# A hybrid attention and convolution block: conv taps as ScalarE products with wide adds, weight sums in place, values two blocks at a time, and seven-product blocks for 6 of 16 pairs

## The chip, the cores and the metric

The kernel runs on one core of one Trainium2 chip. The metric is device time in microseconds (us) of one execution. It is measured as the median of several runs. One more execution is profiled, and all rows of the profile come from that one.

Engine names as in the profile: PE is TensorE (matmul), PEld its weight load, DVE is VectorE, ACT is ScalarE, POOL is GpSimd, SP is SyncE, which issues almost all DMAs.

## The reference

All tensors are float32; the sequence has 256 positions and the model width is 4096.

```
xn = rms_norm(x) * g                                  # (256, 4096)
proj = xn @ w_in                                      # (4096 x 14336)
q, k, v, z_a, a_c, g_c, z_c = split(proj)             # seven parts of 2048
y_a = chunked_attention(q, k, v, rel_table)           # 16 heads of 128, relative bias
y_a = rms_norm(y_a) * silu(z_a)
u   = a_c * sigmoid(g_c)
u   = causal depthwise conv(u, w_dw: 31 taps x 2048 channels) + b_dw
y_c = silu(layer_norm(u)) @ w_pw + b_pw
y_c = rms_norm(y_c) * silu(z_c)
h   = x + concat(y_a, y_c) @ w_out
h   = h + sigmoid(rms_norm(h) @ w_ple_gate + b) * (p @ w_ple)
out = rms_norm(h)
```

## The kernel before

**Products.** Almost all of the time goes into matrix products of a 256-row operand with weights that stream from HBM. A float32 value is split into a high part (rounded to the fp32r type) and a low part (the rest). A product is then three matmuls: high times high, low times high, high times low. For every weight tile of 128 x 1024 values (two column blocks of 512), ACT makes the high part by a cast (`wh`, L197) and DVE makes the low part by a subtraction (`wl`, L198); both are in `parts_of`. PE then reads both.

**`mixed_product`** multiplies the operand by two column blocks at once (2 x 2 outputs of 128 x 512: the 4096 rows of the weight are 16 pairs of 128-row blocks). For a plain pair it issues 2 x 2 x 2 products, that is 24 matmuls. For a pair marked with a star in the order lists (`steady`, `dense`, `early` and so on) it uses a seven-product scheme: 21 matmuls, for which DVE has to form four sums of weight blocks (`ua`, `ub`, L398 to L403) and ACT and DVE have to split these sums too (`uh`, `ul`, through `pair_parts`). The order list `early` marks 4 of 16 pairs.

**Stages.** In order of time: the normalisation and transposition of x together with the first two plain products (block 0 of g and a); then a loop over four blocks g of 512 columns, in which `glu_conv(g + 1)` makes a and g of the next block by one `mixed_product` (in `scaled_pair`) and `heads(g)` makes q and k by another, the values v by a plain `product`, and then runs the attention of four heads; then the layer norm of the convolution (`layer_norm_swish`), the pointwise product, the gates z, the output product, and the gated embedding. The loop over blocks takes about the stretch from 100 to 950 us.

**The convolution** runs on DVE beside these products: `conv_tap` multiplies a 128 x 256 block by one tap's weight and adds it to the accumulator in one instruction (L574; the first tap, with the bias, is L570). There are 4 blocks of 4 x 31 such instructions. They are not issued in one go: they lie in a queue `later`, and `fill(n)` takes n of them after each pair of a product; the input products take 4 per pair, the value product 2.

**Order.** The kernel is recorded by a layer that has its own planner: it may move independent instructions of one engine ahead of others, so the order on an engine is that of the built program and not that of the source. Each engine works strictly through its own order; waits between engines are semaphores.

**Buffers.** Raw weight tiles `wt` have 5 buffers, `wh` and `wl` 3 each, `uh` and `ul` 2 each, the raw sums `ua`/`ub` 2. A DMA for a raw tile is issued (SP) when the tile's last reader is done.

**The layer norm** of the convolution goes over several engines in turn: POOL adds the four blocks and folds them, PE multiplies by a matrix of 1/2048 (the mean, L636), DVE subtracts the mean (`center`, L648), ACT squares (L652), POOL adds and folds the squares (L656, L625, L626), PE makes the variance (L663), and so on. These steps lie in `later` too.

## Time and profile before

| what | value |
|---|---|
| median of 3 runs | 2062.86 us (2062.17 to 2063.23) |
| profiled execution, its own time | 2063.82 us |
| profiled execution, its span | 2061.7 us |
| PE busy | 2034.6 us, 9140 matmuls |
| PEld busy | 1675.2 us |
| DVE busy | 1822.1 us |
| ACT busy | 1152.9 us |
| read from HBM | 406.39 MB |

A row of the groups gives the line, the engine, the operation, the tiles (out<-in), the shapes, the count, then the busy time of the group, the mean duration of one in ns, and the idle time of the engine in front of the group with what ended it. A row of the windows view gives, for one stretch, the busy time (and count) of each engine, the granted TensorE clock, and the share and rate of the DMA engines. A row of the timeline gives start, duration, engine, line, operation and count. Since instructions of one engine overlap a little, the distance between two starts is less than a duration; the distance is what an engine's work adds up from.

### The profile page before, as it was taken

How to read it: one execution, taken by the hardware profiler on the slowest of the kernel's cores; microseconds unless marked ns; L12 is line 12 of the kernel's file. 1: busy time of each engine (PE TensorE's matmuls, PEld its weight loads, DVE VectorE, ACT ScalarE, POOL GpSimd, SP SyncE). 2: the span in 40 equal slices, each digit the busy share in tenths (PEclk: the TensorE clock that was granted, in tenths of full speed). 3: DMA queues.
4: the chain of work that ended last, by engine and by line, in shares of the span. 5: the costliest groups of instructions: out<-in, count | busy, mean ns of one | idle time of the engine just before them, and what ended most of it. 6: DMA issues, size and time to landing. Idle time of an engine off the chain costs nothing.

```text
span 2061.7 us, 25882 instructions
## 1 busy us (share of the span) xinstructions
PE 2034.6 (99%) x9140; PEld 1675.2 (81%) x9140; DVE 1822.1 (88%) x2541; ACT 1152.9 (56%) x1479; POOL 42.9 (2%) x37
## 2 busy tenths in 40 slices
PE   9999999999999999999999999999999999999997
PEld 7888888887888787788888888878888888888886
DVE  7599999899977998875889999899999999999954
ACT  7445535554564535575556656576565666656543
POOL 0000000000000002300000000000000000000000
PEclk9999999999999999999999999999999999999998
DMA  8656665656566665555666666666666656666664
GB/s 291 186 186 201 191 197 184 195 188 188 175 204 185 194 190 164 186 184 195 194 210 202 200 215 197 212 229 206 212 202 206 211 185 192 210 229 210 220 208 166
DMA packets 170331, 412.27 MB, mean 200 GB/s; under 512 B 13006, under 2 KB 16222, under 8 KB 170202
## 3 DMA queue, kind: packets, MB, share of 16 engines
q1 hardware_dynamic: 169914, 410.11, 62.5%
q8 instruction: 71, 1.16, 0.2%
q10 hardware_dynamic: 288, 0.52, 0.1%
q14 instruction: 58, 0.48, 0.1%
HBM read 406.39 MB, written 4.19 MB: 199 GB/s over the span
## 4 chain that ended last, share of the span: by engine, by line
PE 90%; DVE 6%; issue 2%; DMA 1%; ACT 1%; POOL 0%; SPq 0%; ACTq 0%; POOLq 0%; DVEq 0%
PE acc L351 53%; PE acc L210 22%; PE acc_P L351 13%; DVE wl L198 2%; DVE cv L574 1%; PE tmp_ps L156 1%; DVE ul L198 1%; DMA wt<-in_w_in_dram 1%; DMA wt<-in_w_ple_gate_dram 0%; PE tmp_ps L724 0%; PE tmp_ps L739 0%; PE tmp_ps L757 0%; ACT wh L197 0%; DMA xin<-in_x_dram 0%; PE tmp_ps L762 0%
## 5 line engine op out<-in xcount | busy, mean ns | idle before, releaser
L197 ACT CAST wh<-wt 128x1024 fp32r<-128x1024 f32 (+1 forms) x741 | 727.0, 991 | 628.8 <-PE acc L351 319.6
L351 PE MATMUL acc<-wh,big_t 128*128 128x512 f32 x3344 | 1038.8, 391 | 3.4 <-ACT big_t L142 2.9
L198 DVE TENSOR_TENSOR wl<-wt,wh 128x1024 fp32r<-128x1024 f32 (+1 forms) x741 | 850.7, 1159 | 130.2 <-ACT wh L197 127.6
L351 PEld LDWEIGHTS acc<-wh,big_t 128*128 128x128 f32 x3344 | 626.7, 188 | 133.3 <-ACT big_t L142 3.4
L351 PE MATMUL acc<-wl,big_t 128*128 128x512 f32 x1672 | 652.1, 391 | 3.3 <-DVE wl L198 3.2
L210 PE MATMUL acc<-wh,big_t 128*128 128x512 f32 x1248 | 390.2, 393 | 0.0
L351 PEld LDWEIGHTS acc<-wl,big_t 128*128 128x128 f32 x1672 | 314.4, 188 | 71.9 <-DVE wl L198 7.2
L210 PEld LDWEIGHTS acc<-wh,big_t 128*128 128x128 f32 x1248 | 234.9, 189 | 48.2 <-DVE big_t L143 0.2
L210 PE MATMUL acc<-wl,big_t 128*128 128x512 f32 x624 | 243.4, 391 | 0.0
L574 DVE SCALAR_TENSOR_TENSOR cv<-uT,dw,cv 128x256 f32<-128x256 f32 x480 | 214.3, 487 | 1.0
L197 ACT CAST uh<-ub 128x1024 fp32r<-128x1024 f32 x103 | 108.3, 1051 | 113.1 <-DVE ub L403 92.4
L351 PE MATMUL acc_P<-uh,big_t 128*128 128x512 f32 x534 | 163.7, 390 | 0.0
L197 ACT CAST uh<-ua 128x1024 fp32r<-128x1024 f32 x103 | 108.6, 1054 | 63.9 <-DVE ua L399 59.0
L210 PEld LDWEIGHTS acc<-wl,big_t 128*128 128x128 f32 x624 | 117.9, 189 | 24.1
L198 DVE TENSOR_TENSOR ul<-ub,uh 128x1024 fp32r<-128x1024 f32 x103 | 128.2, 1245 | 7.9 <-ACT uh L197 7.1
L198 DVE TENSOR_TENSOR ul<-ua,uh 128x1024 fp32r<-128x1024 f32 x103 | 125.8, 1222 | 0.4
L351 PEld LDWEIGHTS acc_P<-uh,big_t 128*128 128x128 f32 x534 | 99.9, 188 | 21.4 <-ACT uh L197 0.8
L351 PE MATMUL acc_P<-ul,big_t 128*128 128x512 f32 x267 | 103.8, 393 | 0.9 <-DVE ul L198 0.9
L398 DVE TENSOR_TENSOR ua<-wt 128x512 f32<-128x512 f32 x103 | 71.6, 695 | 30.7 <-DMA wt<-in_w_in_dram 17.4
L399 DVE TENSOR_TENSOR ua<-wt 128x512 f32<-128x512 f32 x103 | 70.8, 688 | 4.6 <-DMA wt<-in_w_in_dram 4.3
L403 DVE TENSOR_TENSOR ub<-ub,wt 128x512 f32<-128x512 f32 x103 | 72.2, 701 | 1.2
L402 DVE TENSOR_TENSOR ub<-ua,wt 128x512 f32<-128x512 f32 x103 | 70.9, 688 | 0.2
(199 smaller groups left out, 1349.3 us busy)
## 6 DMA issues: line engine op xcount, KB each, us to landing
wt<-in_w_in_dram SPq DMA_DIRECT2D x447, 512.0 KB, 3.9
wt<-in_w_out_dram SPq DMA_DIRECT2D x128, 512.0 KB, 4.2
wt<-in_w_ple_gate_dram SPq DMA_DIRECT2D x128, 512.0 KB, 4.0
wt<-in_w_pw_dram SPq DMA_DIRECT2D x32, 512.0 KB, 4.3
hc<-in_x_dram SPq DMA_DIRECT2D x8, 512.0 KB, 5.3
wt<-in_w_ple_dram SPq DMA_DIRECT2D x8, 512.0 KB, 4.7
out_dram<-hc SPq DMA_DIRECT2D x16, 256.0 KB, 2.9
xin<-in_x_dram SPq DMA_DIRECT2D x7, 512.0 KB, 8.3
```

Source lines behind the costliest of these rows:

```text
L156: nc.tensor.transpose(pt[:, i * T + h * P : i * T + (h + 1) * P], src[:, h, b * P : (b + 1) * P], ident,)
L197: nc.scalar.copy(wh[:, :kc, :], wt[:, :kc, :]),
L198: nc.vector.tensor_tensor(wl[:, :kc, :], wt[:, :kc, :], wh[:, :kc, :].bitcast(F32), ALU.subtract),
L210: nc.tensor.matmul(acc, a, b[:, k, :], start=kb == 0 and kind == 0, stop=kb == kblocks - 1 and kind == 2,)
L351: nc.tensor.matmul(banks[name], a, b, start=name not in begun, stop=final and ends[name] == n and kind == 2,)
L398: plus(ua[:, 0], w0[:, 0], w0[:, 1])
L399: plus(ua[:, 1], w0[:, 1], w1[:, 1])
L402: plus(ub[:, 0], ua[:, 0], w1[:, 1])
L403: plus(ub[:, 1], ub[:, 0], w1[:, 0])
L574: nc.vector.scalar_tensor_tensor(cv[:, i, :], uT[:, i, k : k + T], dw[:, b, k : k + 1], cv[:, i, :], ALU.mult, ALU.add,)
```

## The change

Five things change.

1. **Convolution.** A tap is no longer one DVE instruction per 128 x 256 block. ACT multiplies each of the four blocks by its tap's weight into a tile `prod` (128 x 4 x n, two buffers), and DVE adds all four at once to the accumulator (`tt`, 128 x 4 x n, n from 255 down to 226). The newest tap, with the bias, is written to the accumulator by ACT directly. The 31 taps of a block are now 32 steps of the queue. In the input products `fill` takes two steps after a plain pair and none after a starred one.
2. **Weight sums in place.** The four sums are written over the raw weight tiles, and the parts of the sums take their buffers from the common `wh`/`wl`, which now have 5 each. The order of the seven products follows.
3. **Values.** v is made for two column blocks at once by `mixed_product` (for g = 0 and g = 2), instead of four plain products, and attention writes its result over v.
4. **Seven products** for 6 of 16 pairs (`early`, and `after_heads` where a product follows an attention) instead of 4 of 16, in all products of the loop over blocks. The sums of x for this cover 6 column blocks instead of 4.
5. **Copies and the layer norm's place.** The PSUM copies of q, k and of the transposed probabilities move from DVE to ACT. The layer norm starts in front of the last q and k product, which takes 8 steps after each plain pair.

In the built program the change has these counts: matmuls of 128 x 512 go from 8619 to 8541; the 496 tap instructions on DVE go away; 496 products of 128 x 256 and less appear on ACT and 120 wide adds on DVE; the starred pairs go from 103 to 129.

```diff
-        return [wpool.tile([P, KC, NB], F32R, tag=tag, name=tag, bufs=3) for tag in ("wh", "wl")]
+        return [wpool.tile([P, KC, NB], F32R, tag=tag, name=tag, bufs=5) for tag in ("wh", "wl")]
...
-    early = units("1 3 5 7 0* 9 2* 11 4* 13 6* 15 8 10 12 14")
+    early = units("1 3 5 0* 7 2* 9 4* 11 6* 13 8* 15 10* 12 14")
+    after_heads = units("1 3 5 7 0* 9 2* 11 4* 13 6* 8* 15 10* 12 14")
...
             w0, w1 = wts
-            ua = upool.tile([P, 2, NB], F32, tag="u", name="ua")
-            ub = upool.tile([P, 2, NB], F32, tag="u", name="ub")
             plus = partial(nc.vector.tensor_tensor, op=ALU.add)
             w0h, w0l = parts_of(w0, 1)[0]
-            plus(ua[:, 0], w0[:, 0], w0[:, 1])
-            plus(ua[:, 1], w0[:, 1], w1[:, 1])
-            uah, ual = pair_parts(ua)
+            plus(w0[:, 0], w0[:, 0], w0[:, 1])
+            plus(w0[:, 1], w0[:, 1], w1[:, 1])
             w1h, w1l = parts_of(w1, 2)[0]
-            plus(ub[:, 0], ua[:, 0], w1[:, 1])
-            plus(ub[:, 1], ub[:, 0], w1[:, 0])
-            ubh, ubl = pair_parts(ub)
+            plus(w1[:, 1], w0[:, 0], w1[:, 1])
+            plus(w1[:, 0], w1[:, 1], w1[:, 0])
+            uah, ual = parts_of(w0, 2)[0]
+            ubh, ubl = parts_of(w1, 2)[0]
...
-    def conv_tap(cv, uT, i, b, k):
-        if k == 0:
-            nc.vector.tensor_scalar(
-                cv[:, i, :], uT[:, i, :T], dw[:, b, 0:1], bdw[:, b : b + 1], ALU.mult, ALU.add
+    def conv_steps(cv, uT, c):
+
+        def scaled(dst, i, n, k, **kw):
+            nc.scalar.activation(
+                dst[:, i, :n], uT[:, i, :n], AF.Identity,
+                scale=dw[:, 4 * c + i, k : k + 1], **kw,
             )
-        else:
-            nc.vector.scalar_tensor_tensor(
-                cv[:, i, :], uT[:, i, k : k + T], dw[:, b, k : k + 1], cv[:, i, :],
-                ALU.mult, ALU.add,
-            )
+
+        def step(k):
+            if waiting:
+                at, n, prod = waiting.pop()
+                tt(cv[:, :, at:], cv[:, :, at:], prod[:, :, :n], ALU.add)
+            if k == PAD:
+                for i in range(4):
+                    scaled(cv, i, T, k, bias=bdw[:, 4 * c + i : 4 * c + i + 1])
+            elif k >= 0:
+                n = T - (PAD - k)
+                prod = taps_pool.tile([P, 4, T], F32, tag="prod", name="prod")
+                for i in range(4):
+                    scaled(prod, i, n, k)
+                waiting.append((PAD - k, n, prod))
+
+        waiting = []
+        return [partial(step, k) for k in range(PAD, -2, -1)]
...
-            sg, gate = scaled_pair(w_in0, o_a + c * NB, o_g - o_a, early, r_x, 4)
+            sg, gate = scaled_pair(
+                w_in0, o_a + c * NB, o_g - o_a, early if c == 1 else after_heads, r_x, (2, 0)
+            )
...
+    def heads(g, splits):
+        last = g == n_g - 1
+        q, k = scaled_pair(
+            w_in0, o_q + g * NB, o_k - o_q, after_heads if last else early, r_x,
+            (8, 0) if last else (2, 0), then=partial(later_memory, splits) if last else None,
+        )
+        qT, kT = to_heads(q, "qT"), to_heads(k, "kT")
+        if g % 2 == 0:
+            v = [act.tile([P, NH, NB], F32, tag="act", name="v") for _ in range(2)]
+            values.extend(scaled_pair(w_in0, o_v + g * NB, NB, early, r_x, (2, 0), dst=v))
...
-        accv = product(w_in0, o_v + g * NB, xT, KD)
-        v = spool.tile([P, NH, NB], F32, tag="hd", name="v", bufs=5)
...
-    xS = [big_tile(upool) for _ in range(2)]
-    for c in range(4):
+    xS = [big_tile(upool) for _ in range(3)]
+    for c in range(6):
```

More of the change, by code (lines that the diff above doesn't have):

```diff
@@ L314, in operand @@
         tiles.append(t)
-    def pair_parts(src):
-        tiles = [upool.tile([P, 2, NB], F32R, tag=tag, name=tag) for tag in ("uh", "ul")]
-        return parts_of(src, 2, tiles)[0]
     def units(text):
@@ L447, in sum_tiles, with scaled_pair @@
         return t, [[t[j][:, h] for j in range(2)] for h in range(NH)]
-    def scaled_pair(w, col, apart, order, r, fills):
-        t, z = sum_tiles()
+    def scaled_pair(w, col, apart, order, r, fills, dst=None, then=None):
+        if dst is None:
+            t, z = sum_tiles()
+        else:
+            t, z = dst, [[dst[j][:, h] for j in range(2)] for h in range(NH)]
         def on_helpers(helper):
@@ L604, in glu_conv @@
             nc.scalar.copy(
[L605 removed]
+                uT[:, 2 * pair : 2 * pair + 2, :], pt.rearrange("q (i t) -> q i t", t=T)
             )
         cv = act.tile([P, 4, T], F32, tag="act", name="cv")
[L608 to L610 removed]
+        later.extend(conv_steps(cv, uT, c))
         conv.append(cv)
@@ L675, in spread @@
                 nc.vector.tensor_scalar(d, ident, st["r"][:, h : h + 1], None, ALU.mult)
-                nc.tensor.matmul(m[:, h * P : (h + 1) * P], mean_w, d, start=True, stop=True)
+                nc.tensor.matmul(m[:, h * P : (h + 1) * P], st["w"], d, start=True, stop=True)
             stat("rs", m[:, :T], float(CW))
@@ L708, in layer_norm_swish @@
             later.extend(partial(swish, c, i) for i in range(4))
-        for c in range(n):
-            later.extend(partial(split, c, i) for i in range(4))
+        return [partial(split, c, i) for c in range(n) for i in range(4)]
     y_a = []
```

80 lines of the change are left out of this document (39 added, 41 removed).

## The prediction

> **What bounds the kernel now.** I read the page first, then the windows of 50 us, the waits of PE, the chain, and the timelines of DVE and ACT.
>
> ```profile
> PE 2034.6 (99%) x9140; PEld 1675.2 (81%) x9140; DVE 1822.1 (88%) x2541; ACT 1152.9 (56%) x1479; POOL 42.9 (2%) x37
> ```
>
> ```profile
> 200.00:250.00 50.00, 49.96 (x221) 41.03 (x220) 50.00 (x74) 27.80 (x30) 0.00 (x0) 1.00 0.64 193
> 250.00:300.00 50.00, 50.00 (x230) 41.46 (x229) 49.63 (x86) 20.01 (x20) 0.00 (x0) 1.00 0.63 196
> ...
> 600.00:650.00 50.00, 50.00 (x226) 41.44 (x225) 34.68 (x40) 26.74 (x30) 0.00 (x0) 1.00 0.66 200
> ```
>
> ```profile
> PEld acc L351 <- DVE wl L198: 7.2, 11, 1.9
> ...
> PEld acc_P L351 <- DVE ul L198: 4.0, 11, 0.9
> ```
>
> ```profile
> 938.64 72.34 PE acc L210 x319
> ```
>
> PE sets the time: 319 matmuls in 72.34 us are 0.2268 us each, and in the loop over blocks it keeps nearly that rate. But DVE is full there too (50.00 and 49.63 of 50 us; in a stretch with few taps left 34.68). PE hardly notices: in the whole run it waits 7.2 + 4.0 us for low parts. Both run side by side at the limit, with some weight tiles made ahead. So whoever gives DVE more work in a stretch than PE has there, and more than the tiles ahead cover, pays on PE.
>
> **Prices.** What an engine's work adds up from is the distance between starts.
>
> ```profile
> 1207.10 1.22 DVE L198 TENSOR_TENSOR wl<-wt,wh 128x1024 fp32r<-128x1024 f32 x1
> 1208.24 0.69 DVE L398 TENSOR_TENSOR ua<-wt 128x512 f32<-128x512 f32 x1
> 1208.84 1.22 DVE L198 TENSOR_TENSOR ul<-ub,uh 128x1024 fp32r<-128x1024 f32 x1
> ```
>
> ```profile
> 177.09 2.06 DVE L574 SCALAR_TENSOR_TENSOR cv<-uT,dw,cv 128x256 f32<-128x256 f32 x5
> ```
>
> ```profile
> 162.14 2.00 ACT L197 CAST wh<-wt 128x1024 fp32r<-128x1024 f32 x2
> ```
>
> ```profile
> L574 DVE SCALAR_TENSOR_TENSOR cv<-uT,dw,cv 128x256 f32<-128x256 f32 x480 | 214.3, 487 | 1.0
> ...
> L461 DVE SCALAR_TENSOR_TENSOR z<-acc,r_x,z 128x512 f32<-128x512 f32 x28 | 19.3, 755 | 3.3 <-PE acc L351 3.3
> ...
> L682 ACT ACTIVATE cv<-cv,prm 128x256 f32<-128x256 f32 x16 | 8.5, 591 | 0.0
> ...
> L570 DVE TENSOR_SCALAR cv<-uT,dw,prm 128x256 f32<-128x256 f32 x16 | 6.4, 417 | 0.2
> ...
> L692 ACT CAST big_t<-cv 128x256 fp32r<-128x256 f32 x16 | 5.2, 405 | 0.0
> ```
>
> A DVE operation on 1024 values takes 1.14 us from start to start, one on 512 takes 0.60; a straight line through both gives 0.07 + n/960. A tap takes 0.40 ((2.06 - 0.49) / 4). Two casts of 1024 take 2.00, so one takes just under 1.0. A wide add isn't in the trace. Its two inputs and shape are those of the 1024 subtraction; with 4 x 241 values on average the line gives 1.07 us. The bounds are 0.60 (the 512 row) and 1.60 (four taps). A product of 256 on ACT lies between the cast of L692 (405 ns) and the swish of L682 (591), that is 0.31 to 0.49 from start to start when the 0.1 us of overlap is taken off; with one per-partition factor where L692 has none and L682 two, I take 0.40.
>
> **The change part by part.**
>
> *Matmuls.* Each starred pair saves three. Nine products with 6 stars replace seven with 4 and four plain ones with none: 54 against 28, 26 x 3 = 78 fewer. PE's path shortens by 78 x 0.2268 = 17.7 us.
>
> *DVE over the loop.* Gone: the taps, 214.3 + 6.4 = 221 us. Added: 120 wide adds, 128; 26 more starred pairs at 4.15 more than a plain one (0.60 for the half tile, 4 x 0.60 for the sums, 3 x 1.14 for the parts make 6.42; a plain pair is 2 x 1.14 = 2.28), 108; final sums and scaling for two more products, about 11; two more column blocks of sums of x, 5; less 19 for the copies that go to ACT. The total grows by about 12 us, while PE loses 17.7. The wide adds pay for the starred pairs and no more.
>
> *Where it lies.* This decides. The source takes 20 steps per product, but in the built program the planner has moved more: 28 adds stand in the first gate product (block 1), 23 in the first q/k product, 9 in the first value product, then 28, 2, 28, 2. In such a product of 28 the middle repeats six times: one plain pair, one starred pair, four adds. On DVE: 2.28 + 6.42 + 4 x 1.07 = 12.98 us. On PE: 45 matmuls, 10.2 us. DVE falls behind by 2.8 each time, 16.6 in six. Before, four repeats with eight taps of 0.40 cost 11.9 against 10.2, 6.8 in four, and that stayed covered.
>
> The cover is the tiles ahead. With five buffers DVE can be four tiles ahead of the one that PE is on: in plain pairs 4 x 12 x 0.2268 = 10.9 us, less one cast and one subtraction (2.1), so 8.8 us. For the starts of the products I added up the built order tile by tile: DVE's work up to each low part, less PE's work up to its first matmul. In the order of before this sum never climbs by more than 7 us in the stretch from 100 to 350 us, which fits a DVE that is full and a PE that doesn't wait. In the changed order it climbs by 20 us in the first gate product and, without a recovery, by 8 more in the first q/k product; then, after a full recovery in the value and gate products, by 22 in the second and by 22 in the third q/k product. Less 8.8 once per climb: 11 + 8 + 13 + 13 = 45 us of waiting on PE. With a cover of 12 it is 35, with 7 it is 55.
>
> *ACT.* In the same products ACT has 6 x 3.4 + 10 x 1.9 for casts, 116 x 0.40 for products and 3 for scaling: 89 us, below DVE's 96. The two buffers of `prod` tie it to DVE's adds, but following one repeat through both orders I find each cast ready as DVE comes to it. Cost nothing; with products at 0.49 ACT would have 99 and would be the bound, 3 to 4 us more in each of the four stretches.
>
> *Weight sums in place.* Same instructions, other order: both sums are formed in front of both casts, so DVE has the other two sums to do while ACT casts. Nothing, while raw tiles arrive in time.
>
> ```profile
> wt<-in_w_in_dram SPq DMA_DIRECT2D x447, 512.0 KB, 3.9
> ```
>
> A raw tile of a starred pair is now held until its sum's low part is made, some 4 us longer (0.60 x 2 + 1.14 x 2 more in front of it), and SP's next load waits for that. The load takes 3.9 us, and a repeat on PE is 10.2; DVE's 8.7 of work in the later stages (no adds) leaves this load about 1 us to spare. I take zero; the rival below prices it.
>
> *Values, copies.* Values are counted above. The copies add 13 us to ACT in places where it has room; attention now needs ACT for one more step, with PE's other matmuls between. Zero.
>
> *Layer norm.* Its place changes. In the last q/k product 8 steps follow a plain pair. In the built order the mean's matmul (L636 before) and the variance's (L663 before) stand 42 full matmuls apart, 9.5 us of PE.
>
> ```profile
> L636 PE MATMUL tmp_ps<-lnsum,mean_w x2: 379/416/454, 838.4 to 838.7; 128*128 128x256 f32 x2
> ```
>
> ```profile
> L648 DVE TENSOR_TENSOR cv<-cv,mu x16: 415/418/2615, 840.4 to 854.5; 128x256 f32<-128x256 f32 x16
> ```
>
> ```profile
> L663 PE MATMUL tmp_ps<-mean_w,sq x4: 250/250/271, 864.8 to 865.2; 128*128 128x1 f32 x4
> ```
>
> ```profile
> 847.71 9.15 POOL L656 TENSOR_TENSOR sq<-sq 128x1024 f32<-128x1024 f32 x2 [44.16 <-ACT sq L652]
> 858.44 2.41 POOL L656 TENSOR_TENSOR sq<-sq 128x1024 f32<-128x1024 f32 x1 [1.58 <-ACT sq L652]
> 860.93 2.15 POOL L625 TENSOR_TENSOR sq<-sq 128x512 f32<-128x512 f32 x1
> 863.16 1.60 POOL L626 TENSOR_TENSOR sq<-sq 128x256 f32<-128x256 f32 x1
> ```
>
> Before, the way from the one to the other took 26.4 us (838.4 to 864.8), with enough matmuls between. In the changed order DVE does its 16 subtractions in one go, so the way shortens: 0.7 for the mean, 2.7 for the first two blocks, 1.1 to square, then POOL's 9.15 + 2.41 + 2.15 + 1.60, together 19.8. PE waits 19.8 - 9.5 = 10 us, in order, and so do the casts that stand behind the squares on ACT. Bounds: 5 (POOL's two long adds at 2.41 each) and 15 (a way as slow as before).
>
> Beside DVE's subtractions POOL needs 9.15 us for two of its adds, and 2.41 for the third. [...]
>
> *Clock.* PE's waits can cost twice.
>
> ```profile
> 500.67 0.33 PE L724 MATMUL tmp_ps<-ident,z 128*128 128x128 f32 x1 [1.35 <-DVE z L461]
> ```
>
> ```profile
> 500.00:505.00 5.00, 4.00 (x18) 3.63 (x19) 4.35 (x7) 0.17 (x1) 0.00 (x0) 0.66 0.27 97
> ```
>
> After a gap of 1.35 us and thin work the granted clock of these 5 us was 0.66: if it was halved, for 3.4 us, which is 1.7 us of PE time. I add one such loss after the layer norm's wait, 1.7; in the stretches where DVE is the bound a slow PE is hidden. [...]
>
> *Waits that go.* Of the 11.2 us that PE waits for low parts before, those outside the four stretches may go: I take 5 off.
>
> *Sum,* against the profiled execution's 2063.8 us: - 17.7 + 45 + 10 + 1.7 - 5 = 2097.8. The median of the runs is 1.0 lower (2062.86), so 2097 us.
>
> **The rivals.**
>
> *Faster: DVE's shortfall stays under the cover.* If a wide add costs 0.65 or less, the repeat costs 11.3, six fall short by 6.6, and that is covered as before. Against it: between the 512 and the 1024 row DVE needs (1.14 - 0.60) / 512 = 1.05 ns a value, whatever the operation's length. For it: the bound 0.60, and a PE that tolerates a full DVE for 250 us now. Then 17.7 and most of 11.2 are gained and the layer norm costs 7: 2063.8 - 17.7 - 11 + 7 - 1 = 2041 us.
>
> *No change:* a cover of 13 (all five tiles) and a layer norm that costs 5 or less, with all old waits gone, bring the shortfall to some 20 to 25 and the time to 2059 to 2067.
>
> *Slower by ACT:* products at 0.49, plus 16: 2113 us.
>
> *Slower by the raw tiles:* if each of the 75 starred pairs behind the loop waits 0.5 us for its load, plus 37: 2134 us. Against it: DVE would have to use up its spare time and its tiles ahead first.
>
> **How the numbers follow.** The forecast has 0.66, its own range 2066 to 2122; ACT 0.05 and the raw tiles 0.04; the faster rival 0.18, spread over 2033 to 2055; no change 0.07. Two in a thousand, 4 us, is about what a measurement of this kernel can tell. Faster 0.18, same 0.07, slower 0.75. The range from 2044 to 2122 leaves out half of the faster rival and the top.
>
> **What would show it.** In the profile after: the wide adds at about 1.1 us; DVE at 50 of 50 in the windows of the first gate and the first three q/k products, with PEld under 40 there and waits of PE and PEld for `wl` of 40 us or more in total; the variance's matmul with a wait of about 10 us for POOL; no loss from about 950 us on, so that the end of the loop moves by as much as the total. Wrong it is if PE's waits for `wl` stay near 11 us, or if the time comes or goes behind the loop.

## The result: slower by 3.1%, and the profile after

| what | before | after |
|---|---|---|
| median of the runs | 2062.52 us (2061.94 to 2063.23, 4 runs) | 2125.84 us (2125.51 to 2126.86, 4 runs) |
| profiled execution, its span | 2061.7 us | 2123.6 us |

The ratio is 1.0308 (95% interval 1.0290 to 1.0326). The forecast of 2097 us had the direction and most of the mechanism, but the change costs 63 us where it said 34; the time lies 4 us above the range.

The page's first part, the windows of 50 us in the same stretches as before, and the waits of TensorE and of its weight loads:

```profile
PE 2043.5 (96%) x9062; PEld 1656.8 (78%) x9062; DVE 1875.3 (88%) x2317; ACT 1392.4 (66%) x2063; POOL 41.6 (2%) x33
```

```profile
150.00:200.00 50.00, 42.30 (x171) 30.85 (x172) 49.34 (x55) 44.88 (x83) 0.00 (x0) 1.00 0.52 165
200.00:250.00 50.00, 49.40 (x221) 39.94 (x219) 49.37 (x55) 44.27 (x77) 0.00 (x0) 1.00 0.58 182
250.00:300.00 50.00, 43.79 (x183) 32.61 (x182) 49.35 (x55) 44.66 (x82) 0.00 (x0) 1.00 0.59 190
500.00:550.00 50.00, 44.81 (x176) 33.08 (x174) 49.58 (x53) 43.64 (x83) 0.00 (x0) 0.94 0.53 168
600.00:650.00 50.00, 50.00 (x229) 41.29 (x230) 41.22 (x50) 30.05 (x41) 0.00 (x0) 1.00 0.49 151
```

```profile
PEld acc_P L347 <- ACT wh L196: 57.6, 43, 3.3
PE acc_P L347 <- ACT wh L196: 38.8, 42, 2.8
PEld acc_P L347 <- DVE wl L197: 20.8, 40, 1.1
```

In the windows of the first gate product and the first two q/k products DVE is at 49.3 to 49.6 of 50, and PE falls to 42 to 45 of 50 in three of the four; in the light product from 600 us on PE is full again. TensorE waits for weight parts of starred pairs (`acc_P`), by name more often for the high part than for the low one. That doesn't make ACT the bound: the high part of a sum can be cast only when DVE has formed the sum. The repeat of a plain pair, a starred pair and four adds shows it, in TensorE's and the page's rows:

```profile
127.21 0.73 PE L347 MATMUL acc_P<-wh,big_t 128*128 128x512 f32 x2 [1.00 <-ACT wh L196]
140.47 0.73 PE L347 MATMUL acc_P<-wh,big_t 128*128 128x512 f32 x2 [1.00 <-ACT wh L196]
153.67 0.73 PE L347 MATMUL acc_P<-wh,big_t 128*128 128x512 f32 x2 [1.00 <-ACT wh L196]
166.79 0.74 PE L347 MATMUL acc_P<-wh,big_t 128*128 128x512 f32 x2 [1.00 <-ACT wh L196]
179.86 0.73 PE L347 MATMUL acc_P<-wh,big_t 128*128 128x512 f32 x2 [1.00 <-ACT wh L196]
```

```profile
L572 ACT ACTIVATE prod<-uT,dw 128x255 f32<-128x255 f32 (+14 forms) x480 | 195.7, 486 | 25.7 <-DVE cv L580 25.0
L580 DVE TENSOR_TENSOR cv<-cv,prod 128x1020 f32<-128x1020 f32 (+14 forms) x120 | 138.4, 1154 | 18.5 <-ACT prod L572 16.5
```

The distance from start to start is 13.1 to 13.3 us where 12.98 was forecast, against 10.2 us of matmuls. Each repeat loses 2.9. A wide add has a mean duration of 1154 ns and a product on ACT one of 486; from start to start both are a little shorter (1.10 to 1.11 us from the adds at 494.65 and 496.37 us to the next operation, 0.40 us for each of 20 products that take 8.05).

To see where TensorE's time goes I added up, from the trace, how far each matmul starts later than 0.227 us after the one ahead of it. Before, this is 33.7 us in all; after, 109.0:

| stretch, us | before | after | forecast, waits that come or go |
|---|---|---|---|
| 100 to 200 (first gate product) | 1.3 | 17.4 | 11 |
| 225 to 300 (first q/k) | 0.5 | 9.9 | 8 |
| 475 to 600 (second q/k and what precedes it) | 4.3 | 21.6 | 13 |
| 675 to 800 (third q/k and what precedes it) | 4.2 | 20.6 | 13 |
| layer norm to last scaling (800 to 950 before, 850 to 1000 after) | 6.2 | 21.5 | 10 |
| from 1000 us on | 7.6 | 10.2 | 0 |

75.3 us more of waiting less 17.7 us of matmuls is 57.6; the span grew by 61.9. Most of the 4 us between are starts that are late by less than 0.05 us, 2.6 us more of them than before, which the sum leaves out. Matmuls at a halved clock (0.94 on average in the window from 500 us, 0.50 from 499 to 505) start late too, 0.43 us after the one ahead as at 702.64 and 703.07 us, and so they stand in the table: 9.3 us of the 109.0, 2.1 of the 33.7 before.

### The profile page after: what moved, and what is told of

It reads as the page before. It is cut to its first block, busy times and chain, and to the rows that moved or that the text cites. A ratio compares the mean times of both kernels' runs of the same rounds, so it can differ in the third digit from the quotient of the medians.

```text
span 2123.6 us, 26357 instructions
## 1 busy us (share of the span) xinstructions
PE 2043.5 (96%) x9062; PEld 1656.8 (78%) x9062; DVE 1875.3 (88%) x2317; ACT 1392.4 (66%) x2063; POOL 41.6 (2%) x33
## 4 chain that ended last, share of the span: by engine, by line
PE 80%; DVE 8%; ACT 7%; issue 3%; DMA 2%; POOL 1%; ACTq 0%; DVEq 0%; POOLq 0%
PE acc L347 52%; PE acc_P L347 13%; PE acc L209 12%; DVE wl L197 4%; ACT wh L196 3%; ACT prod L572 3%; DMA wt<-in_w_in_dram 2%; DVE cv L580 1%; DVE wt L393 1%; PE tmp_ps L155 1%; POOL sq L672 1%; PE tmp_ps L755 0%; DVE wt L396 0%; PE tmp_ps L773 0%; DVE big_t L709 0%
## 5 line engine op out<-in xcount | busy, mean ns | idle before, releaser
L196 ACT CAST wh<-wt 128x1024 fp32r<-128x1024 f32 (+1 forms) x999 | 962.5, 994 | 594.5 <-DVE wt L394 203.8
L197 DVE TENSOR_TENSOR wl<-wt,wh 128x1024 fp32r<-128x1024 f32 (+1 forms) x999 | 1124.8, 1155 | 139.5 <-ACT wh L196 126.6
L347 PE MATMUL acc<-wh,big_t 128*128 128x512 f32 x3802 | 1174.4, 392 | 7.7 <-ACT wh L196 4.1
L347 PE MATMUL acc_P<-wh,big_t 128*128 128x512 f32 x948 | 299.4, 398 | 38.8 <-ACT wh L196 38.8
L347 PEld LDWEIGHTS acc_P<-wh,big_t 128*128 128x128 f32 x948 | 175.8, 189 | 91.7 <-ACT wh L196 57.6
L209 PE MATMUL acc<-wh,big_t 128*128 128x512 f32 x736 | 230.9, 395 | 0.1
L572 ACT ACTIVATE prod<-uT,dw 128x255 f32<-128x255 f32 (+14 forms) x480 | 195.7, 486 | 25.7 <-DVE cv L580 25.0
L347 PE MATMUL acc_P<-wl,big_t 128*128 128x512 f32 x474 | 186.2, 400 | 7.1 <-DVE wl L197 6.7
L580 DVE TENSOR_TENSOR cv<-cv,prod 128x1020 f32<-128x1020 f32 (+14 forms) x120 | 138.4, 1154 | 18.5 <-ACT prod L572 16.5
L347 PEld LDWEIGHTS acc_P<-wl,big_t 128*128 128x128 f32 x474 | 88.3, 190 | 37.4 <-DVE wl L197 20.6
L393 DVE TENSOR_TENSOR wt<-wt 128x512 f32<-128x512 f32 x129 | 90.9, 705 | 2.9
L396 DVE TENSOR_TENSOR wt<-wt 128x512 f32<-128x512 f32 x129 | 88.9, 689 | 3.3
L397 DVE TENSOR_TENSOR wt<-wt 128x512 f32<-128x512 f32 x129 | 88.9, 689 | 3.2
L394 DVE TENSOR_TENSOR wt<-wt 128x512 f32<-128x512 f32 x129 | 89.2, 692 | 0.5
L470 ACT ACTIVATE junk<-hc 128x512 bf16<-128x512 f32 x32 | 20.1, 630 | 22.3 <-DVE hc L176 12.7
```

Of the source, the lines that this page charges most:

```text
L196: nc.scalar.copy(wh[:, :kc, :], wt[:, :kc, :]),
L197: nc.vector.tensor_tensor(wl[:, :kc, :], wt[:, :kc, :], wh[:, :kc, :].bitcast(F32), ALU.subtract),
L209: nc.tensor.matmul(acc, a, b[:, k, :], start=kb == 0 and kind == 0, stop=kb == kblocks - 1 and kind == 2,)
L347: nc.tensor.matmul(banks[name], a, b, start=name not in begun, stop=final and ends[name] == n and kind == 2,)
L393: plus(w0[:, 0], w0[:, 0], w0[:, 1])
L394: plus(w0[:, 1], w0[:, 1], w1[:, 1])
```

## The experiments

Runs that share a chip were measured against the kernel before on that chip; its median was 2061.8 to 2063.2 throughout.

| run | what | us | ratio to before, 95% |
|---|---|---|---|
| e1 | taps left out but the newest | 2059.94 | 0.9977 to 1.0000 |
| e2 | wide adds left out | 2067.49 | 1.0013 to 1.0036 |
| e3 | steps held behind the newest weight part | 2114.33 | 1.0214 to 1.0274 |
| e4 | as e3, one step after every pair | 2112.00 | 1.0203 to 1.0263 |
| e5 | as e3, a later start | 2112.51 | 1.0230 to 1.0266 |
| e6 | as e3, four stars | 2100.49 | 1.0168 to 1.0201 |
| e7 | as e3, the norm's last steps (the splits) and its places moved | 2111.36 | 1.0221 to 1.0254 |
| e8 | e6 and e7 together | 2090.36 | 1.0115 to 1.0151 |
| e9 | after, four buffers | 2148.77 | 1.0408 to 1.0439 |
| e10 | as e3, half of the adds | 2113.68 | 1.0239 to 1.0273 |
| e11 | as e3, adds on GpSimd | 2201.49 | 1.0661 to 1.0693 |
| e12 | e8, the norm's additions on VectorE | 2079.12 | 1.0073 to 1.0103 |
| e13 | as e3, no adds | 2112.60 | 1.0229 to 1.0257 |
| e14 | after, first six steps held | 2128.52 | 1.0302 to 1.0334 |
| e15 | after, the norm's additions on VectorE | 2122.49 | 1.0275 to 1.0303 |
| e16 | **before**, the norm's additions on VectorE | 2055.97 | 0.9957 to 0.9980 |
| e17 | after, a later start, nothing held | 2107.24 | 1.0195 to 1.0229 |
| e18 | e15, splits after the attention | 2121.36 | 1.0268 to 1.0299 |

### Which part costs: the taps, and of these the adds (e1, e2)

```diff
-        return [partial(step, k) for k in range(PAD, -2, -1)]
+        return [partial(step, PAD)]                                       # e1
```
```diff
-                tt(cv[:, :, at:], cv[:, :, at:], prod[:, :, :n], ALU.add)   # e2
```

> The changed kernel with only the newest tap of the convolution: the 30 other taps (480 ScalarE products and 120 wide adds) are left out. Theory A (the conv steps fill DVE and ACT in four products): DVE then has 67 us of work in a product where PE has 83 to 86, so PE's waits in the four stretches (about 70 us) go and only the layer norm's and the attention's remain: 2060 to 2070 us. Theory B (weight sums in place make raw tiles late): the taps don't matter much, above 2100 us.

> The changed kernel with all 480 products on ScalarE but without the 120 wide adds on DVE. Theory A1 (DVE's queue is the bound in the middle of a product, ACT's burst of products at the start of a block empties the cover): the repeats run at PE's pace, the starts of blocks still wait: 2065 to 2085 us. Theory A2 (ACT's products ahead of the casts are the bound): most of the loss stays, above 2100 us.

Without taps the change takes 2060 us: all the rest of it, starred pairs, sums in place, two value products, the norm's new place, is worth 2.5 us, at the edge of the noise. In e1 TensorE's waits from 775 to 950 us, around the norm, are 22.3 us, 8.1 before; so most of what the 78 matmuls save goes there. The taps cost 66 us. Of these the products on ACT cost 7.6 and the adds on DVE 58. The windows of e2:

```profile
100.00:200.00 100.00, 99.91 (x448) 81.87 (x447) 79.97 (x89) 95.99 (x177) 0.00 (x0) 1.00 0.61 193
200.00:300.00 100.00, 100.00 (x450) 82.86 (x449) 81.24 (x89) 99.94 (x185) 0.31 (x1) 1.00 0.61 195
```

ACT at 96 and 99.9 of 100 leaves PE full as long as DVE has 20 us to spare. The rivals "slower by ACT" and "slower by the raw tiles" fall here.

### Spreading the steps, and why that test wasn't one (e3, e4, e10, e13)

Each step is placed behind the cast and the subtraction that were recorded last, so that the planner can't draw steps together; e4 also takes one step after every pair, e10 leaves out every other add, e13 all.

```diff
+    newest = []
...
-        made = (
+        made = newest[:] = (
...
+        def placed(k):
+            with tc.issue_after(newest[0].ins), tc.issue_after(newest[1].ins):
+                step(k)
+
-        return [partial(step, k) for k in range(PAD, -2, -1)]
+        return [partial(placed, k) for k in range(PAD, -2, -1)]
```

> The changed kernel with one thing more: each conv step is held behind the two casts and subtractions of the weight part made last before it in the source, so that the planner can't move it ahead. All computation is there. The built order then has 18, 18, 20, 4, 18, 12, 18, 12 adds in the eight products, in place of 28, 23, 9, 0, 28, 2, 28, 2, and no burst of 20 products. Theory A: DVE has at most 87 us where PE has 86, the four stretches lose 10 us or less in all: 2065 to 2080 us, what remains being the layer norm's 20. Theory B: no change, 2115 to 2126.

> As the run before, but one step after every pair, starred or not, in place of two after each plain one: 14 or 16 adds in each of the eight products. Theory A: no product has more DVE work than PE work except those with an attention beside them (88 against 93): 2062 to 2075 us, 3 to 8 below the run before. Theory B: no change, 2115 to 2126.

> The run with held tap steps (2114.3 us) with every other wide add left out (60 of 120 are made; all 480 products are made). Without any adds the time was 2067.5, so the 120 adds cost 47 us when they are spread. Theory 'VectorE has a little time left in each product and only what goes beyond it is paid for': the first half is nearly free and 2069 to 2082 us comes out. Rival 'every add costs TensorE the same, about 0.4 us': 2088 to 2094 us. Between 2083 and 2087 us the run doesn't tell them apart.

> The run with held tap steps with all 120 wide adds left out (all 480 products made, at the held places). With all adds it took 2114.3 us and with half of them 2113.7. Reading of that: in a repeat of a plain and a starred pair VectorE has 8.7 us of work and stands 1.2 us idle while ScalarE casts the last sum made in place (the sum may be written only after the low part of the raw tile, the cast only after the sum); a second add fills that idle time, so it costs nothing. Without any add the repeat is under TensorE's 10.2 us: 2064 to 2074 us. Rival 'holding the tap products behind the newest weight part makes ScalarE late by itself': 2095 to 2114 us with casts that TensorE waits for.

e3 and e4 recovered 12 and 14 us where 46 to 64 were expected. I read that at first as an add that costs the same wherever it lies, which was wrong: with half of the adds left out the time stayed (2113.7), and with none it stayed again (2112.6). e13 differs from e2 only in that the products are held, and is 45 us slower. So the holding costs 45 us by itself, as e13's rival said, and e3 to e8 and e10 to e12 say nothing on what spread adds would cost. What it does is seen in one repeat of e13, in the timelines of ACT and DVE (the brackets hold the idle time ahead and what ended it):

```profile
206.21 3.15 ACT L574 ACTIVATE prod<-uT,dw 128x232 f32<-128x232 f32 x8
...
217.47 3.13 ACT L574 ACTIVATE prod<-uT,dw 128x230 f32<-128x230 f32 x8
220.50 1.56 ACT L198 CAST wh<-wt 128x512 fp32r<-128x512 f32 x2
224.41 1.05 ACT L198 CAST wh<-wt 128x1024 fp32r<-128x1024 f32 x1 [2.35 <-DVE wt L396]
225.86 2.94 ACT L198 CAST wh<-wt 128x1024 fp32r<-128x1024 f32 x3 [0.40 <-DVE wt L399]
```

```profile
221.14 0.69 DVE L199 TENSOR_TENSOR wl<-wt,wh 128x512 fp32r<-128x512 f32 x1 [1.95 <-ACT wh L198]
221.87 0.69 DVE L395 TENSOR_TENSOR wt<-wt 128x512 f32<-128x512 f32 x1
222.48 1.22 DVE L199 TENSOR_TENSOR wl<-wt,wh 128x1024 fp32r<-128x1024 f32 x1
223.61 0.69 DVE L396 TENSOR_TENSOR wt<-wt 128x512 f32<-128x512 f32 x1
```

The held products stand right in front of the first cast of a starred pair. DVE waits 1.95 us for that cast, then ACT waits 2.35 us for the sum. With sums in place this is one chain: cast of the raw half, its low part, the sum written over it, the cast of the sum. Neither engine is full (DVE 72 to 74 of 100 and ACT 81 to 84 in the windows between 100 and 300 us), but they wait for each other, and the repeat takes 11.26 us (206.21 to 217.47) against 10.2 on PE.

### Fewer stars and the layer norm, on the held version (e5 to e8, e11, e12)

```diff
+        later.extend([lambda: None] * 6 + conv_steps(cv, uT, c))          # e5
-        later.extend(conv_steps(cv, uT, c))
```
```diff
-    early = units("1 3 5 0* 7 2* 9 4* 11 6* 13 8* 15 10* 12 14")         # e6; after_heads alike
+    early = units("1 3 5 7 0* 9 2* 11 4* 13 6* 15 8 10 12 14")
```
```diff
-            (8, 0) if last else (2, 0), then=...                           # e7; the splits go
+            (4, 4) if last else (2, 0), then=...                           # behind the attention
```
```diff
-                tt(cv[:, :, at:], cv[:, :, at:], prod[:, :, :n], ALU.add)   # e11
+                nc.gpsimd.tensor_tensor(cv[:, :, at:], cv[:, :, at:], prod[:, :, :n], ALU.add)
```
```diff
-        add = nc.gpsimd.tensor_tensor                                      # e12: e6 + e7 + this
+        add = nc.vector.tensor_tensor
```

> Everything is computed. As the run with each tap step held behind the weight part made last before it (2114.3 us), and the six first places after the start of a block's window carry no tap step, so that VectorE and ScalarE go on making weight parts while TensorE is still at the tail of the previous product; the same 18 or so adds then fall in the later part of the window. Theory 'the cover of 8.8 us is real but is spent at the start of each window, where the engines wait for one another in the first tap steps': the start is used for weight parts again, 4 to 8 us come back in five windows each minus what the denser remainder costs, 2085 to 2104 us. Rival 'each wide add costs about 0.5 us wherever it lies, since the whole alternation has no VectorE time left': the adds are only moved, and 2110 to 2120 us comes out. Below 2085 us neither holds.

> Everything is computed. As the run with held tap steps (2114.3 us), with four pairs of seven products in each input projection in place of six: two more pairs of 16 made of eight products, so 26 x 2 matmuls come back per starred pair taken away, 12.2 us in all by the rows of 0.2345 us a matmul, and one sum step of 2.7 us less of VectorE per pair taken away. Theory 'VectorE is full where starred pairs and wide adds alternate': some 55 us of TensorE's idle time in the loop falls to 10 to 20 us, 2078 to 2092 us. Rival 'the adds cost the same wherever they lie': the matmuls come on top, 2118 to 2127 us. Rival 'ScalarE holds it': casts of a plain and a starred pair are equally many, so the idle time stays and 2115 to 2127 us comes out too; then ScalarE's busy share in the windows tells the two apart.

> Everything is computed. As the run with held tap steps (2114.3 us), with two edits around the layer norm: the 16 steps that split its result into two parts are issued from the queue after the last attention and not inside the last q/k product, and that product's tap and norm work is spread over plain and starred pairs (4 and 4 places) in place of plain pairs alone (8 and 0). Theory 'the splits stand ahead of the final scaling and of the casts, and this is the 8.5 us near 950 us that the forecast left out': 8 to 13 us come back, 2101 to 2106 us. Rival 'the splits are only moved and delay the first weight parts after the attention by as much': 2111 to 2117 us, with the idle time at another place.

> Everything is computed. The held tap steps, four starred pairs in place of six and the edits around the layer norm together. If the three causes (full alternation, order of the window's start, splits ahead of the last scaling) are separate, the gains add: the run with four starred pairs less 8 to 13 us, 2066 to 2084 us. If idle time taken away in one place only shows up as a wait at the next, it ends within 4 us of the run with four starred pairs alone. Below 2060 us it would be ahead of the kernel before.

> Everything is computed. The run with held tap steps (2114.3 us) with all 120 wide adds on GpSimd in place of VectorE. Theory 'VectorE's time is what the adds cost': 138 us leave VectorE, GpSimd has 15 adds of 2.4 to 3.3 us in a product of some 86 us and ends in time, 2067 to 2080 us. Rival 'GpSimd's additions hold up VectorE's operations while they run' (in the run with four starred pairs VectorE's subtraction took 3.36 us in place of 1.22 and its wide add 3.30 in place of 1.10 beside an addition on GpSimd): each add then costs VectorE some 2 us in place of 1.15, 100 us more of VectorE over the loop, 2150 to 2220 us.

> Everything is computed. The run with held tap steps, four starred pairs and the edits around the layer norm (2090.4 us), with the layer norm's ten additions (six of 1024 values, two of 512, two of 256) on VectorE in place of GpSimd. There TensorE lost 8.6 us between 750 and 775 us, beside three additions on GpSimd of 2.7 to 2.9 us each. Theory 'GpSimd's additions hold up VectorE': that loss falls to 2 or 3 us, and the way to the variance shortens too, 2080 to 2086 us. Rival 'VectorE is simply full there': ten operations more on it, 8.6 us, 2090 to 2099 us.

e5 gained 1.8 us, within the noise and in its rival's range, but for the reason above. e6 is 14 us faster with 54 matmuls (12 us at 0.227 each) more (9116 against 9062 in the pages; two starred pairs in each of nine products, three matmuls each), so some 26 us of waiting went with two starred pairs per product, less than the theory's 35 to 45. e7 gained 3 and e8 10 against e6. e11 is the clear one: 87 us slower than e3, in its rival's range.

```profile
158.38 4.44 POOL L582 TENSOR_TENSOR cv<-cv,prod 128x984 f32<-128x984 f32 x2 [8.51 <-ACT prod L574]
```

```profile
161.07 2.29 DVE L395 TENSOR_TENSOR wt<-wt 128x512 f32<-128x512 f32 x1
164.42 0.68 DVE L396 TENSOR_TENSOR wt<-wt 128x512 f32<-128x512 f32 x1
```

While two additions run on POOL, DVE's sum of 512 values takes 2.29 us; the next one, without POOL, 0.68. In all VectorE isn't busier than with the adds on itself. Against e3, by the groups, it is rid of the adds (140.7 us) and needs 101 us more for two others: the subtractions (L199) take 1174.4 us where they took 1129.6, and the first sums of the 129 starred pairs (L395) 144.7 where they took 88.9. These 56 us (mean 1122 ns, 689 in e3) stand in the chain of e13; that this place is why the kernel is slower is read from the trace, not shown by a run. Slow additions that keep ScalarE from a free `prod` buffer are not it: ScalarE waits 7.2 us for GpSimd in all. e12 goes the other way: it took 11.2 us off e8 by the medians, 9.9 when each is set against the kernel before on its own chip, the upper end of its theory's 4 to 10.

### Where the cover went (e9, e14, e17)

```diff
-        return [wpool.tile([P, KC, NB], F32R, tag=tag, name=tag, bufs=5) for tag in ("wh", "wl")]
+        return [wpool.tile([P, KC, NB], F32R, tag=tag, name=tag, bufs=4) for tag in ("wh", "wl")]   # e9
```
```diff
-        return [partial(step, k) for k in range(PAD, -2, -1)]
+        return [partial(placed if k > PAD - 6 else step, k) for k in range(PAD, -2, -1)]           # e14
```
```diff
-        later.extend(conv_steps(cv, uT, c))
+        later.extend([lambda: None] * 6 + conv_steps(cv, uT, c))                                   # e17
```

> Everything is computed. The changed kernel (2125.8 us) with four buffers in place of five for the high and low weight parts, so that one tile fewer can lie ready. The forecast's model (each of the four long climbs of VectorE's work is covered by the tiles ahead before TensorE waits): one tile less is 12 matmuls, 2.7 us, per climb, 11 us more in all, 2137 us; in stretches where the cover was enough before, more. Rival 'the tiles ahead have been spent by the start of each climb, because ScalarE's burst of tap products stops the casts and VectorE waits behind it': the fifth buffer lies empty while VectorE is the bound, 2124 to 2130 us.

> Everything is computed. The changed kernel (2125.8 us) in which only the first six tap steps of a block are held behind the weight part made last before them, so that ScalarE no longer makes the bias step and up to five products in one burst of 8 to 10 us at the start of a product; 28 adds still stand in the second and third q/k product. Theory 'the tiles ahead, worth up to 8.8 us, are spent by that burst': the wait of 3 us at the start of those products goes and 5 to 8 us come back at each of four starts, 2096 to 2108 us. Rival 'there is no cover to speak of: VectorE is behind from the first starred pair on': only the waits at the start go, 2115 to 2124 us.

> Everything is computed. The changed kernel (2125.8 us) with six empty places in the queue ahead of each block's tap steps and nothing held. In the built order ScalarE now makes a cast after every one or two groups of four products at the start of a product, where the run that held the first six steps still had up to 20 products in a row. The wide adds per product become 24, 23, 13, 0, 21, 9, 21, 9, so VectorE's climbs shrink by about 4, 0, 7 and 7 us. Theory 'the tiles that lie ready when the starred pairs begin are short: the four tiles of a starred pair last TensorE 21 matmuls, 4.8 us, not 4 x 2.72, so hardly 2.7 us of cover are left, burst or no burst': only the smaller climbs come back, 2104 to 2116 us. Rival 'the burst spends a cover of 7 to 9 us at each of four starts': 28 us more come back, 2076 to 2092 us.

How long a weight tile lies ready can be worked out from the trace: from the end of the subtraction to the first matmul that reads the low part. In the kernel after, the subtraction that ends at 480.8 us is read 9.3 us later. So the cover was there, and larger than the forecast's 8.8. The next subtraction ends at 493.0 and is read 0.1 us later. These are the two matmuls that read them:

```profile
490.07 0.39 PE L347 MATMUL acc<-wl,big_t 128*128 128x512 f32 x1
493.05 0.50 PE L347 MATMUL acc_P<-wl,big_t 128*128 128x512 f32 x1
```

Between the two stand these rows of ACT and DVE in the kernel after:

```profile
481.13 2.08 ACT L572 ACTIVATE cv<-uT,prm,dw 128x256 f32<-128x256 f32 x4
483.11 8.05 ACT L572 ACTIVATE prod<-uT,dw 128x255 f32<-128x255 f32 x20
491.06 1.56 ACT L196 CAST wh<-wt 128x512 fp32r<-128x512 f32 x2
```

```profile
479.56 1.23 DVE L197 TENSOR_TENSOR wl<-wt,wh 128x1024 fp32r<-128x1024 f32 x1
484.84 1.22 DVE L580 TENSOR_TENSOR cv<-cv,prod 128x1020 f32<-128x1020 f32 x1 [4.06 <-ACT prod L572]
492.31 1.82 DVE L197 TENSOR_TENSOR wl<-wt,wh 128x512 fp32r<-128x512 f32 x2
```

ACT makes 24 tap operations in a row, 10 us without a cast, and DVE stands idle for 4.06 us and then waits between adds. e14 was to take that burst away and didn't: its built order has it still, and the time is that of the kernel after, within the noise; so it tests neither theory.

```profile
483.96 8.05 ACT L574 ACTIVATE prod<-uT,dw 128x255 f32<-128x255 f32 x20
```

In e17 it is gone; ACT alternates:

```profile
480.02 1.04 ACT L196 CAST wh<-wt 128x1024 fp32r<-128x1024 f32 x1
480.96 1.71 ACT L572 ACTIVATE prod<-uT,dw 128x255 f32<-128x255 f32 x4
482.56 1.03 ACT L196 CAST wh<-wt 128x1024 fp32r<-128x1024 f32 x1
```

e17 takes 2107.2 us, in the theory's range and far from the rival's. The waits in the four climbs fall from 69.5 to 49.3 us, 5.8 of that beside the norm's additions near 780 us; without these, 43.5. The smaller climbs, as they were worked out before the run, account for some 18 of the 26 us. That leaves about 8 for the burst, not 28; a part of these 8 may be clock, which in the kernel after is at 0.50 for 6.8 us in the second and in the third climb; over the whole execution its mean is 0.990 there and 0.992 in e17. And the cover now lasts as expected of short tiles. These are the subtractions of the first starred pair's first and last tile and of the second one's last tile (of a row of four, the first), and the matmuls that read them:

```profile
477.87 0.69 DVE L197 TENSOR_TENSOR wl<-wt,wh 128x512 fp32r<-128x512 f32 x1 [1.50 <-ACT wh L196]
488.15 4.09 DVE L197 TENSOR_TENSOR wl<-wt,wh 128x1024 fp32r<-128x1024 f32 x4
500.33 4.10 DVE L197 TENSOR_TENSOR wl<-wt,wh 128x1024 fp32r<-128x1024 f32 x4
```

```profile
488.37 0.39 PE L347 MATMUL acc_P<-wl,big_t 128*128 128x512 f32 x1
491.77 0.39 PE L347 MATMUL acc_P<-wl,big_t 128*128 128x512 f32 x1
501.97 0.39 PE L347 MATMUL acc_P<-wl,big_t 128*128 128x512 f32 x1
```

The first is made at 478.6 us and lies ready for 9.8 us, the second is made at 489.4 and lies for 2.4, and the third, made at 501.6, for 0.4. So the four tiles of one starred pair, with three adds beside them, use up three quarters of the lead, and in the third pair TensorE waits (first at 512.6 us). A plain tile feeds 12 matmuls, 2.72 us; the four tiles of a starred pair feed 21 together, 4.8 us. By the forecast's own working, four tiles ahead less one cast and one subtraction, five buffers that hold a starred pair are worth 4.8 - 2.1 = 2.7 us, not 8.8. e9 missed on both sides (23 us): 7.7 us of it lie in the climbs, 1 to 2 us in three of them and 4 in the first q/k (a tile of a sum feeds 1.4 us, a plain one 2.7); 10.7 lie behind 1000 us, where five buffers carry stretches that four don't. It tells that the fifth buffer is worth something in the climbs, not which theory holds.

### The layer norm (e15, e16, e18)

e15 and e16 are the one line of e12, in the kernel after and in the kernel before. e18 is e15 with the splits issued after the last attention.

> Everything is computed. The changed kernel (2125.8 us) with the layer norm's ten additions on VectorE in place of GpSimd, nothing else. In the run with four starred pairs and held steps this took 11.2 us off. Theory 'an addition on GpSimd holds up VectorE by more than it would take there, and lies in the chain from the mean to the variance, where TensorE waits 10 us by the forecast': 2111 to 2118 us, and the gaps of 4.2 and 4.5 us around the variance's matmul fall below 2 us each. Rival 'VectorE is full there, so ten more operations cost their 8.6 us': 2128 to 2135 us.

> Everything is computed. The kernel before (2062.5 us) with the layer norm's ten additions on VectorE in place of GpSimd, nothing else. Before, TensorE loses 8.2 us between 775 and 950 us, with VectorE 88 to 94% busy. If GpSimd's additions hold up VectorE there too, 2057 to 2061 us, ahead of both kernels; if the loss there comes from VectorE's own work, 2062 to 2067 us.

> Everything is computed. The changed kernel with the layer norm's additions on VectorE (2122.5 us), and the 16 steps that split its result issued after the last attention and not inside the last q/k product. In the run with the additions alone TensorE's loss fell from 13 to 5 us between 850 and 925 us and rose from 8.5 to 12 us between 950 and 1000 us. Theory 'what is left there is the splits, which stand ahead of the last scaling on VectorE and ScalarE': 9 to 12 us come back, 2110 to 2114 us. Rival 'they only meet the weight parts after the attention': 2118 to 2124 us.

In the kernel after, TensorE's waits around the variance's matmul come to 13.0 us, near the 10 of the forecast. They are the two of 4.07 us below, and starts at a halved clock (0.50 from 899 to 908 us) behind them; the wait of 5.15 us for the last scaling (L461) was not in the forecast:

```profile
885.82 5.45 DVE L664 TENSOR_TENSOR cv<-cv,mu 128x256 f32<-128x256 f32 x16
889.76 11.70 POOL L672 TENSOR_TENSOR sq<-sq 128x1024 f32<-128x1024 f32 x3 [5.18 <-ACT sq L668]
895.78 1.06 ACT L668 ACTIVATE sq<-cv 128x1024 f32<-128x1024 f32 x1 [4.20 <-POOL sq L672]
897.83 0.50 PE L347 MATMUL acc<-wh,big_t 128*128 128x512 f32 x1 [4.07 <-ACT wh L196]
903.66 1.01 PE L679 MATMUL tmp_ps<-mean_w,sq 128*128 128x1 f32 x4 [4.07 <-POOL sq L640]
973.24 1.54 PE L739 MATMUL tmp_ps<-ident,z 128*128 128x128 f32 x6 [5.15 <-DVE z L461]
```

e15 gains 3.4 us, not 8 to 15: between 850 and 925 us the waits fall from 13.0 to 5.2, and between 925 and 1000 they rise from 8.5 to 13.0. The loss moved. e18 took the splits out of the way of the last scaling and gained 1.1 us more, within the noise and in its rival's range; its waits in the two stretches are 6.7 and 12.5. There ACT does the norm's 16 last activations in one run of 8.00 us, and the next cast of a weight part stands behind it at 959.40 us:

```profile
949.67 8.00 ACT L698 ACTIVATE cv<-cv,prm 128x256 f32<-128x256 f32 x16
957.56 1.94 ACT L455 ACTIVATE z<-z,r_x 128x512 f32<-128x512 f32 x3
959.40 1.03 ACT L196 CAST wh<-wt 128x1024 fp32r<-128x1024 f32 x1
```

That such runs of 16 are what is left is argued, not shown.

e16 makes the kernel before faster: 2055.97 us (2054.86 to 2057.43, 6 runs), 0.3% ahead, and so ahead of both kernels. That is small but clear of noise (0.9957 to 0.9980), and a little more than the 1.5 to 5.5 us expected.

```profile
PE 2029.4 (99%) x9140; PEld 1672.4 (81%) x9140; DVE 1815.5 (88%) x2551; ACT 1152.6 (56%) x1479; POOL 15.7 (1%) x27
```

```profile
L648 DVE TENSOR_TENSOR cv<-cv,mu x16: 418/421/423, 833.7 to 847.9; 128x256 f32<-128x256 f32 x16
```

DVE has ten operations more and is busy for 6.6 us less (1822.1 before). The longest of the 16 subtractions takes 423 ns where it took 2615. TensorE's waits fall from 33.7 to 27.0 us, 4.5 of this between 775 and 950 us. Before, the clock was halved twice for 3.4 us elsewhere, and its mean was 0.996; in this execution it is 0.997.

## Why the forecast was too low, step by step

- **78 matmuls, 17.7 us:** the count is right (9140 less 9062), and e1, which carries it, is 2.5 us ahead of before although TensorE waits 14 us longer around the norm there.
- **Prices, and the repeat of 12.98 us:** right; 13.1 to 13.3 us a repeat, and 20 products on ACT in 8.05 us are the 0.40 us taken.
- **ACT at nothing:** right as a bound (e2). But its order counted: the burst at the start of a product, about 8 us in all.
- **The cover of 8.8 us, taken off each climb:** this step failed. Climbs of 20, 8, 22 and 22 us, 72 in all, cost 17.4, 9.9, 21.6 and 20.6, 69.5 in all where 45 was forecast. The tiles ahead were counted at a plain tile's 2.72 us each. In starred pairs, where the climb happens, they are short (2.7 us of cover by the same working), and before the climb starts the burst empties them. The bounds of this step were too narrow as well: with a cover of 7 the climbs leave 13 + 8 + 15 + 15 = 51 and not 55, and no cover that was considered reaches 69.5. For "no change" a cover of 13 leaves 33, so that rival had less ground than it was given.
- **Sums in place, nothing:** nothing in e1 and e2, which carry them and are as fast as before or nearly so. The chain that they make shows once ACT's casts are late (e13). From the same matmul near 1000 us to the end the kernel after takes 2.5 us longer than before; the raw-tile rival's 37 us aren't there.
- **Layer norm, 10 us:** the waits around the variance were 13.0 after. The 8.5 us near 950 us were left out; with both, 15 us more than before where 10 was forecast. The step on POOL's price held (11.70 us for three additions beside DVE, 11.56 by its rows).
- **Clock, 1.7 us:** too small. The granted clock was 0.50 for 30.6 us in four stretches (three of 6.8 us and one of 10.2), where it was for 6.8 us in two before (the last microseconds of a run left out), and starts that are late by it come to 9.3 us against 2.1. Of the 7 us between, 5.6 lie in the second and third climb; how much of these TensorE would have waited for weight parts anyway is not shown.
- **Waits that go, 5 us:** they don't; the waits in the same stretches are in the table, and none fell by that much.

In sum, 28 us were missing (61.9 less 34). The four stretches make 19 of them (59 us more than before, where 45 less 5 was forecast): the cover, the waits that didn't go, and what of the clock lies there. The layer norm with its splits makes 5 and the stages behind 1000 us 2.6; the last 1 us is what the table doesn't count, less the 1.7 that were put in for the clock.

Of the signs that the prediction named, the wide add's price and the DVE and PEld windows came as said. The waits for `wl` didn't: PE's and PEld's come to 30 us where 40 or more were named, and the larger ones go by `wh`. And from 950 us on there was a loss.

Left open is what 120 adds would cost in a light, even spread without holds; e17 goes a part of the way.

## What to carry to other kernels

When an engine falls behind, count the cover in the consumer's time of the tiles that lie in the buffers at that moment, not in that of the longest tile: a scheme that saves matmuls makes its tiles shorter, and so its own cover smaller (here 4.8 us of TensorE for the four tiles of a starred pair, 10.9 for four plain ones). An experiment that holds instructions in place adds waits of its own (45 us here), so run it once with the suspected work left out as well; here that run (e13) changed the reading of nine others. And look for small work on an engine that holds up the full one while it runs, as GpSimd did here: ten additions moved from GpSimd to a VectorE that was 88% busy made the kernel 6.3 us faster.

## What the runs showed of the hardware

Additions on GpSimd held up VectorE's sums and subtractions beside them: a sum of 0.68 us took 2.29 (e11), a subtraction of 0.42 us up to 2.62 (the kernel before). The norm's ten additions cost VectorE more that way than when it did them itself: moved to VectorE (e16), they left it busy for 6.6 us less, and the kernel before was 6.3 us faster. The 120 additions of e11 cost it less, 101 us against 140.7, but, as the trace reads, at a worse place, and the kernel was 87 us slower.

The granted clock was 0.50 for 3.4 us after gaps of TensorE of 1.35 and 1.77 us in the kernel before (so from 502 to 504.9 and from 1345 to 1348 us), both beside short matmuls of 128x128. In the kernel after it was 0.50 for 6.8 to 10.2 us in or after gaps of 2.84 (twice), 4.07 and 5.15 us (so from 499 to 505, 697 to 703, 899 to 908 and 970 to 976 us). After gaps of 1.47 us before and of 1.32 and 1.59 us after, these two beside short matmuls as well, it stayed at 1.00. So in these two executions the length of a gap alone doesn't tell whether the clock fell.
